# Attention scores: the low part of the keys stored on all 128 partitions

## The chip, the core and the metric

One Trainium2 chip, one of its cores. The metric is the device time of one execution in microseconds. The engines named below are TensorE (PE, its weight loads are listed apart as PEld), VectorE (DVE), ScalarE (ACT), GpSimd (POOL), and SyncE (SP), whose queue issues most of the loads from memory.

## The reference, cut to what matters

Two layers, 256 latent and 256 context tokens of width 1024. Each layer projects the tokens, runs three token mixers (attention, convolution, pooling) side by side, merges them, and ends in a mixture of 16 experts. The part of interest is the score product of the attention, with 8 query heads in two groups of 4, each group sharing one of 2 key heads of size 64:

```
s_win = jnp.einsum('bnqkgd,bnskd->bnkgqs', qb, kw)     # latent queries, latent keys in a band
s_ctx = jnp.einsum('bnqkgd,blkd->bnkgql', qb, k_ctx)   # latent queries, context keys
s     = jnp.einsum('blkgd,bmkd->bkglm', qg, k)         # context queries, context keys (layer 0 only)
```

All of it is in float32, and a softmax with one extra "sink" column follows.

## The kernel before

Products that need more accuracy than one pass of TensorE's fast float32 form gives are made from split operands. A value x is kept as a high part (x rounded to that form) and a low part (x minus the high part). The projections (helper `mm3`, lines 492 to 499) are three passes over such halves, eight matmuls each, all with weights of 128 rows.

For the scores a trick is used, since a head has only 64 dimensions and the array has 128 rows. In the tile of queries, `QS` for the latent and `QC` for the context tokens, 64 partitions of a head hold the high part of q and the other 64 hold its low part (lines 544 to 549). `KS` holds the high part of the keys twice, once on each half (lines 560 and 561). One matmul over all 128 rows so adds q_high times k_high and q_low times k_high. The low part of the keys, `KL`, is written by line 562 on the 64 partitions of its key head alone; a second matmul, with the 64 rows of q_high as weights, adds q_high times k_low.

`scores(s, qb, kv)` does one group of 4 heads for 128 queries. For context queries (s = 1) a head takes a pair of matmuls with 256 columns, lines 591 and 592. For latent queries (s = 0) it takes a triple: lines 596 and 597 with 512 columns, and line 598, a 128x128 bf16 product that adds the mask. Each result goes to one of four PSUM banks called `ax`; DVE takes the row maximum (601) and the softmax offset (603), ACT the exponential (606). `weigh` then scales the probabilities (624 on ACT, 626 on DVE) and transposes them on PE (631, evicted by 633), and `values` multiplies by v (644, 648, 649).

Layer 0 has 4 groups with s = 1 and 4 groups with s = 0, so 16 pairs and 16 triples; layer 1 has 4 groups with s = 0, so 16 triples. Between `scores` and `weigh` of a group the program puts one or two units of the convolution's projection (`conv_units`, lines 496 to 499) and some taps of the convolution on DVE (`pump_taps`, lines 474 and 478). A scheduler then sets the order on each engine, with the splits of the weights (lines 238 and 239) drawn ahead by a priority. Each engine works through its list in that order.

After the mixers come the output projection (872), the routing and the experts (1080, 1103, 1108). Their weights, 12 MB for each expert, are loaded by SP's queue into tiles as these come free (`prefetch`, line 355).

Of the kernel before, what the change touches and what calls it, by code (L numbers as in the profile page):

```python
# [10 lines left out]
F32 = mybir.dt.float32  # L11
F32R = mybir.dt.float32r
# [7 lines left out]
NH, NKV, HD, WIN = 8, 2, 64, 128  # L20
# [107 lines left out]
def dit_block(ctx: ExitStack, tc: tile.TileContext, out, kcv, kb16, rope_in, tok, cols, w_mod0, w_mod,  # L128
              b_mod, w_in, w_attn_o, w_conv_o, w_pool, w_pool_o, w_out, w_router,
              w_e, final_norm_g):  # L130
    nc = tc.nc

    def opened(name, bufs, side="left", **kw):
        g = tc.tile_pool(name=name, bufs=bufs, side=side, reuse_waits="tile", **kw)
        return g, g.__enter__()
# [9 lines left out]
    def bank(tag, dt=F32):  # L145
        pool, bufs = psum[tag]
        return pool.tile([128, 512], dt, tag=tag, name=tag, bufs=bufs)
# [19 lines left out]
    def t2(name, n=512, dt=F32):  # L167
        return L.tile([128, n], dt, tag="t2", name=name, bufs=6)
# [32 lines left out]
    def small(shape, name, bufs=2, dt=F32):  # L201
        return P0.tile(shape, dt, tag=name, name=name, bufs=bufs)
# [8 lines left out]
    for l in range(DEPTH):  # L211
# [8 lines left out]
        gdr, DR = opened(f"dr{l}", 1, side="right")  # L220
# [280 lines left out]
        def unit(src, n, view="p (k n) -> p k n", eng="v", **kw):  # L501
            w = split(src, view, eng, **(kw or dict(k=8)))
            w = [v.rearrange("p (k n) -> p k n", k=8) for v in w]
            ps = bank("mm")
            mm3(ps[:, :n], w, (hh, hl), 8, n)
            nunit[0] += 1
            if nunit[0] % MOD_EVERY[l] == 0:
                pump_mod()
            return ps
# [4 lines left out]

        QS = DR.tile([128, NH, 256], F32R, tag="qf", name="QS")
        KS = DR.tile([128, NKV, 512], F32R, name="KS")
        KL = DR.tile([128, 512], F32R, name="KL")
        if NS == 2:
            QC = big("E", "QC", F32R)[:, :2048].rearrange("p (h n) -> p h n", h=NH)
        sides = (slice(0, 64), slice(64, 128))  # L520
# [12 lines left out]
        for u in range(2):  # L533
            tv = qw.pop() if qw else qload(u)
            for v in range(2):
# [8 lines left out]
                for kv in range(2):  # L544
                    hp, ho = sides[kv], sides[1 - kv]
# [9 lines left out]
        kf = t2("kf")  # L555
        roped(kf[:, 0:256], ps)
        nc.scalar.activation(kf[:, 256:512], ps[:, 256:512], AF.Copy)
        for kv in range(2):
            hp, ho = sides[kv], sides[1 - kv]
            nc.scalar.activation(KS[hp, kv, :], kf[hp], AF.Copy)  # L560
            nc.vector.tensor_copy(KS[ho, kv, :], kf[hp])
            nc.vector.tensor_sub(KL[hp], kf[hp], KS[hp, kv, :].bitcast(F32))
        ps = unit(kvw[:, :, 128:256], 512, eng=LOW["v"][l])
        vf = t2("vf", 512)
        nc.scalar.activation(vf, ps, AF.Copy)
# [5 lines left out]
        def prt(name):  # L571
            return DR.tile([128, 2 * 272], F32, tag="pr", name=name, bufs=4)
# [7 lines left out]
        def scores(s, qb, kv):  # L580
            nk = 4 if s == 0 else 2
            q0 = 128 * qb
            hp = sides[kv]
            nm = small([128, 4], "nm")
            rs = small([128, 4], "rs")
            pr4 = []
            for i in range(4):
                sc = bank("ax")
                if s == 1:
                    q = QC[:, 4 * kv + i, q0:q0 + 128]  # L590
                    nc.tensor.matmul(sc[:, :256], q, KS[:, kv, 256:512], start=True, stop=False)
                    nc.tensor.matmul(sc[:, :256], q[hp], KL[hp, 256:512], start=False, stop=True)
                else:
                    kb = 1 - qb
                    q = QS[:, 4 * kv + i, q0:q0 + 128]
                    nc.tensor.matmul(sc, q, KS[:, kv, :], start=True, stop=False)
                    nc.tensor.matmul(sc, q[hp], KL[hp], start=False, stop=False)
                    nc.tensor.matmul(sc[:, kb * 128:(kb + 1) * 128], identb, maskb[:, qb, :],
                                     start=False, stop=True)
                mx = small([128, 1], "mx")  # L600
                nc.vector.reduce_max(mx, sc[:, :nk * 128], axis=AX.X)
                hs = 4 * kv + i
                nc.vector.tensor_scalar(nm[:, i:i + 1], mx, -(HD ** -0.5), nsink[:, hs:hs + 1],
                                        op0=ALU.mult, op1=ALU.min)
                pr = prt("pr")
                nc.scalar.activation(pr[:, :nk * 128], sc[:, :nk * 128], AF.Exp, scale=HD ** -0.5,
                                     bias=nm[:, i:i + 1], accum_out=rs[:, i:i + 1])
                pr4.append(pr)
            hs = 4 * kv
            es = small([128, 4], "es")  # L610
            nc.vector.tensor_add(es, nm, sink[:, hs:hs + 4])
            nc.scalar.activation(es, es, AF.Exp)
            nc.vector.tensor_add(rs, rs, es)
            nc.vector.reciprocal(rs, rs)
            return pr4, rs
# [62 lines left out]
        for s in reversed(range(NS)):  # L678
            for qb in range(2):
                if s == 0:  # L680
                    pT = A[1:]
                else:
                    p1 = A[2]
                    pT = [p1[:, :1024], p1[:, 1024:]]
                pT = [p.rearrange("p (k i n) -> p k i n", i=4, n=128) for p in pT]
                for kv in range(2):
                    pr4, rs = scores(s, qb, kv)
                    for _ in range(2 // NS):
                        next(fill, None)
                        pump_taps(TAPS["attn"][l])  # L690
                    weigh(s, kv, pT, pr4, rs)
                values(s, qb, pT)
# [340 lines left out]
        for e in range(NE):  # L1033
# [36 lines left out]
            for i in range(4):  # L1070
                wg, wu = [eload().rearrange("p (k n) -> p k n", k=2) for _ in range(2)]
                for kk in range(2):
                    k = 2 * i + kk
                    for f in range(2):
                        for u, w in enumerate((wg, wu)):
                            if NS == 2:
                                o = pgu[f][64 * u:64 * u + 64, :]
                            else:
                                o = pgu[0][64 * u + 32 * f:64 * u + 32 * f + 32, :]
                            nc.tensor.matmul(o, xeT[k // 4][:, k % 4, e, :], w[:, kk, 512 * f:512 * f + 512],  # L1080
                                             start=k == 0, stop=k == 7)
# [118 lines left out]
```

## Time and profile before

| | |
|---|---|
| median of 3 runs | 1712.94 us (1711.73 to 1713.78) |
| the profiled execution | 1712.34 us, its span 1710.5 us |
| PE busy | 1483.2 us (87%), 7788 matmuls |
| DVE busy | 670.3 us (39%) |
| ACT busy | 407.6 us (24%) |
| DMA, mean over the span | 310 GB/s |
| mean granted clock of TensorE | 0.941 |

A busy PE is not a PE at its peak: a matmul's record begins when it is given to the array and its end is modelled, so the gap between the starts of two neighbours says more than a record's own length. The attention of layer 0 stands at about 82 to 190 us of the span, that of layer 1 at about 1022 to 1081 us.

### The profile page before, as it was taken

How to read it: one execution, taken by the hardware profiler on the slowest of the kernel's cores; microseconds unless marked ns; L12 is line 12 of the kernel's file. 1: busy time of each engine (PE TensorE's matmuls, PEld its weight loads, DVE VectorE, ACT ScalarE, POOL GpSimd, SP SyncE). 2: the span in 40 equal slices, each digit the busy share in tenths (PEclk: the TensorE clock that was granted, in tenths of full speed). 3: DMA queues.
4: the chain of work that ended last, by engine and by line, in shares of the span. 5: the costliest groups of instructions: out<-in, count | busy, mean ns of one | idle time of the engine just before them, and what ended most of it. 6: DMA issues, size and time to landing. Idle time of an engine off the chain costs nothing. (4 is left out here: it accounts for less than half of the span.)

```text
span 1710.5 us, 19121 instructions
## 1 busy us (share of the span) xinstructions
PE 1483.2 (87%) x7788; PEld 802.1 (47%) x7788; DVE 670.3 (39%) x1137; ACT 407.6 (24%) x760; POOL 232.4 (14%) x234
## 2 busy tenths in 40 slices
PE   6999989999999999999998899999979765666575
PEld 3665667888654433333332267789844111111111
DVE  3568993352553221121211268975542110111011
ACT  3455312232432100000000257434421000000001
POOL 0300430154740000000000020325100000000000
PEclk9999999999999999999999999999989887878878
DMA  9643435234546999999999865566689999999996
GB/s 398 230 173 130 148 144 207 75 139 181 197 176 255 425 428 427 428 426 428 428 407 428 334 242 179 196 225 229 268 336 429 427 429 427 428 427 428 428 428 258
DMA packets 48185, 530.01 MB, mean 310 GB/s; under 512 B 5345, under 2 KB 6113, under 8 KB 7906
## 3 DMA queue, kind: packets, MB, share of 16 engines
q1 hardware_dynamic: 46224, 526.10, 75.8%
q10 hardware_dynamic: 1874, 2.70, 0.5%
q8 instruction: 61, 1.00, 0.2%
q14 instruction: 26, 0.21, 0.0%
HBM read 527.73 MB, written 1.05 MB: 309 GB/s over the span
## 5 line engine op out<-in xcount | busy, mean ns | idle before, releaser
L1080 PE MATMUL mm<-we,xeT 128*32 128x512 f32 (+1 forms) x1880 | 347.1, 662 | 97.8 <-DMA we<-in_w_e_dram 97.8
L1080 PEld LDWEIGHTS mm<-we,xeT 128*32 128x32 f32 (+1 forms) x1880 | 95.1, 129 | 337.5 <-issue 190.2
L496 PE MATMUL mm<-hh,ws 128*128 128x512 f32 (+1 forms) x672 | 221.8, 349 | 0.3
L497 PE MATMUL mm<-hl,ws 128*128 128x512 f32 (+1 forms) x672 | 218.6, 344 | 0.5 <-DVE hl L430 0.4
L238 ACT ACTIVATE ws<-w 128x1024 fp32r<-128x1024 f32 x132 | 139.3, 1058 | 303.6 <-PE mm L499 202.5
L1087 DVE TENSOR_TENSOR hm<-si,mm 64x512 f32<-64x512 f32 x48 | 33.1, 690 | 405.8 <-ACT si L1085 271.4
L1085 ACT ACTIVATE si<-mm 64x512 f32<-64x512 f32 x48 | 28.3, 590 | 684.9 <-PE mm L1080 684.9
L478 DVE SCALAR_TENSOR_TENSOR acc<-up,dw,acc 128x512 f32<-128x512 f32 (+1 forms) x240 | 156.7, 693 | 1.1
L239 DVE TENSOR_TENSOR ws<-w,ws 128x1024 fp32r<-128x1024 f32 x94 | 122.3, 1304 | 70.5 <-ACT ws L238 70.2
L496 PEld LDWEIGHTS mm<-hh,ws 128*128 128x128 f32 x672 | 127.3, 190 | 29.2 <-issue 12.6
L497 PEld LDWEIGHTS mm<-hl,ws 128*128 128x128 f32 x672 | 127.4, 190 | 18.6 <-issue 3.5
L499 PE MATMUL mm<-hh,ws 128*128 128x512 f32 (+1 forms) x672 | 132.7, 339 | 1.0 <-DVE ws L239 0.9
L239 POOL TENSOR_TENSOR ws<-w,ws 128x1024 fp32r<-128x1024 f32 x38 | 97.2, 2564 | 211.2 <-ACT ws L238 211.2
L1103 PE MATMUL mm<-we,hT 128*64 128x512 f32 x432 | 111.2, 639 | 5.0 <-ACT hT L1098 4.8
L499 PEld LDWEIGHTS mm<-hh,ws 128*128 128x128 f32 x672 | 107.1, 189 | 15.9 <-DVE ws L239 2.1
L1045 POOL COPY sel<-kc 48x128 f32<-48x128 f32 (+1 forms) x16 | 4.6, 285 | 799.8 <-DVE hm L1087 428.8
L1115 DVE TENSOR_TENSOR Y<-mm,G 32x512 f32<-32x512 f32 x64 | 44.0, 687 | 135.8 <-PE mm L1103 135.0
L1108 PE MATMUL mm<-we,hT 128*32 128x512 f32 x424 | 69.1, 762 | 11.6 <-DMA we<-in_w_e_dram 9.6
L1103 PEld LDWEIGHTS mm<-we,hT 128*64 128x64 f32 x432 | 33.5, 146 | 76.5 <-issue 66.1
L1125 PE MATMUL ax<-Y,sg 128*128 128x512 f32 x128 | 58.4, 603 | 8.8 <-DVE Y L1118 6.4
L1118 DVE TENSOR_TENSOR Y<-mm,G 64x512 f32<-64x512 f32 x32 | 22.0, 688 | 96.1 <-PE mm L1108 95.7
L1095 PE MATMUL ax<-kc,hm 64*128 64x64 f32 x192 | 32.6, 294 | 31.0 <-DVE hm L1087 30.2
(260 smaller groups left out, 1715.3 us busy)
## 6 DMA issues: line engine op xcount, KB each, us to landing
we<-in_w_e_dram SPq DMA_DIRECT2D x166, 2048.0 KB, 26.6
w<-in_w_mod_dram SPq DMA_DIRECT2D x44, 1024.0 KB, 5.3
w<-in_w_in_dram SPq DMA_DIRECT2D x42, 1024.0 KB, 4.9
A<-in_w_e_dram SPq DMA_DIRECT2D x20, 2048.0 KB, 23.2
w<-in_w_out_dram SPq DMA_DIRECT2D x12, 1024.0 KB, 4.9
we<-in_w_e_dram SPq DMA_DIRECT2D x10, 1024.0 KB, 17.3
wm<-in_w_mod_dram SPq DMA_DIRECT2D x4, 1024.0 KB, 18.0
w<-in_w_attn_o_dram SPq DMA_DIRECT2D x4, 1024.0 KB, 4.9
```

What stands on the lines that cost most here:

```text
L238: nc.scalar.activation(h, src, AF.Copy)
L239: (nc.gpsimd if eng == "p" else nc.vector).tensor_sub(lw, src, h.bitcast(F32))
L478: nc.vector.scalar_tensor_tensor(acc[:, ch], up[:, ch, :, k:k + 256], dw[:, 4 * k + ch:4 * k + ch + 1], acc[:, ch], op0=ALU.mult, op1=ALU.add)
L496: nc.tensor.matmul(ps, wh[:, k, :], ah[:, k, :n], start=k == 0, stop=False)
L497: nc.tensor.matmul(ps, wh[:, k, :], al[:, k, :n], start=False, stop=False)
L499: nc.tensor.matmul(ps, wl[:, k, :], ah[:, k, :n], start=False, stop=k == nk - 1)
L1080: nc.tensor.matmul(o, xeT[k // 4][:, k % 4, e, :], w[:, kk, 512 * f:512 * f + 512], start=k == 0, stop=k == 7)
L1087: nc.vector.tensor_mul(hm[0:64, :], si[0:64, :], pgu[f][64:128, :])
L1103: nc.tensor.matmul(pd[64 * h:64 * h + 64, :], hT[:, 64 * k:64 * k + 64], rhs, start=k == 0, stop=k == 7)
L1108: nc.tensor.matmul(pd[o:o + 32, :], hT[:, c0:c0 + 32], rhs, start=k < 2, stop=k >= 6)
L1115: nc.vector.tensor_mul(Y[b0:b0 + 32, s, cols], pd[rw, :], G2[l][rw, :])
L1125: nc.tensor.matmul(po, sgs[s][:, t * 128:(t + 1) * 128], Y[:, s, cols], start=True, stop=True)
```

## The change

`KL` becomes one 128-partition block for each key head. Line 562 writes the half it wrote before, a new line 563 writes the same difference on the other half, and both score matmuls of a head take the whole 128-row query tile as weights. The second product so adds q_low times k_low as well.

```
-        KL = DR.tile([128, 512], F32R, name="KL")
+        KL = DR.tile([128, NKV, 512], F32R, name="KL")
...
-            nc.vector.tensor_sub(KL[hp], kf[hp], KS[hp, kv, :].bitcast(F32))
+            nc.vector.tensor_sub(KL[hp, kv, :], kf[hp], KS[hp, kv, :].bitcast(F32))
+            nc.vector.tensor_sub(KL[ho, kv, :], kf[hp], KS[hp, kv, :].bitcast(F32))
...
-            hp = sides[kv]
...
-                    nc.tensor.matmul(sc[:, :256], q[hp], KL[hp, 256:512], start=False, stop=True)
+                    nc.tensor.matmul(sc[:, :256], q, KL[:, kv, 256:512], start=False, stop=True)
...
-                    nc.tensor.matmul(sc, q[hp], KL[hp], start=False, stop=False)
+                    nc.tensor.matmul(sc, q, KL[:, kv, :], start=False, stop=False)
```

On PE, ACT, POOL and SP the instructions stand in the order they had. DVE gets two more subtractions in each layer. In layer 0 they stand between the casts of the high keys (`KS`) and the split of the next weights (`ws`), as this piece of the difference of DVE's list shows (- before, + after):

```order
 L561 CAST KS<-kf 64x512 x2
-L562 TENSOR_TENSOR KL<-kf,KS 64x512 x2
-L239 TENSOR_TENSOR ws<-w,ws 128x1024
-L569 COPY vt<-ax 128x512
+L562 TENSOR_TENSOR KL<-kf,KS 64x512
+L563 TENSOR_TENSOR KL<-kf,KS 64x512
+L562 TENSOR_TENSOR KL<-kf,KS 64x512
+L563 TENSOR_TENSOR KL<-kf,KS 64x512
+L239 TENSOR_TENSOR ws<-w,ws 128x1024
+L570 COPY vt<-ax 128x512
```

Both halves of key head 0 are now written before the first of key head 1, and the split and the copy of v (`vt`) stand behind four subtractions in place of two.

In layer 1 no split stands between them and the copy of v, after which come the row maxima of the first scores; this is the same place of DVE's list there:

```order
 L239 TENSOR_TENSOR ws<-w,ws 128x1024
 L561 CAST KS<-kf 64x512 x2
-L562 TENSOR_TENSOR KL<-kf,KS 64x512 x2
-L569 COPY vt<-ax 128x512
+L562 TENSOR_TENSOR KL<-kf,KS 64x512
+L563 TENSOR_TENSOR KL<-kf,KS 64x512
+L562 TENSOR_TENSOR KL<-kf,KS 64x512
+L563 TENSOR_TENSOR KL<-kf,KS 64x512
+L570 COPY vt<-ax 128x512
```

The copy of v moves behind two more subtractions, and with it the maxima that follow.

## Rows read from the trace of the kernel before

**Rows 1.** Stretches: width; busy of PE, PEld, DVE, ACT, POOL; clock; DMA share, GB/s.
```profile
82.00:120.00 38.00, 38.00 (x171) 25.57 (x170) 25.64 (x68) 20.82 (x63) 0.00 (x0) 1.00 0.43 146
127.00:172.00 45.00, 43.74 (x208) 25.94 (x205) 38.42 (x74) 25.95 (x55) 2.39 (x1) 1.00 0.35 126
1020.00:1075.00 55.00, 55.00 (x359) 39.40 (x358) 45.48 (x105) 42.36 (x84) 0.15 (x2) 1.00 0.44 152
1400.00:1700.00 300.00, 194.91 (x1067) 47.00 (x1060) 39.62 (x59) 14.29 (x31) 2.43 (x5) 0.81 0.98 415
```

**Rows 2.** Chain that ended last, in order of time: start, us, what.
```profile
1023.79 0.43 PE ax L597
...
1651.84 37.13 DMA we<-in_w_e_dram
```

**Rows 3.** Groups by line, weight loads: busy, mean ns, idle before, what ended it.
```profile
L496 PEld LDWEIGHTS mm<-hh,ws 128*128 128x128 f32 x672 | 127.3, 190 | 29.2 <-issue 12.6 <-ACT ws L238 1.0 <-ACT pr L624 0.8
...
L597 PEld LDWEIGHTS ax<-KL,QS 64*128 64x128 f32 x32 | 5.8, 183 | 8.6 <-issue 8.6
...
L592 PEld LDWEIGHTS ax<-KL,QC 64*128 64x128 f32 x16 | 2.9, 183 | 2.5 <-issue 1.0
```

**Rows 4.** Timeline of PE, triples of layer 0: start, us, what.
```profile
128.45 0.50 PE L597 MATMUL ax<-KL,QS 64*128 64x512 f32 x1
128.88 0.23 PE L598 MATMUL ax<-bt 128*128 128x128 bf16 x1
128.92 0.48 PE L596 MATMUL ax<-KS,QS 128*128 128x512 f32 x1
129.33 0.50 PE L597 MATMUL ax<-KL,QS 64*128 64x512 f32 x1
...
131.74 0.23 PE L598 MATMUL ax<-bt 128*128 128x128 bf16 x1
131.78 0.48 PE L497 MATMUL mm<-hl,ws 128*128 128x512 f32 x1
132.09 0.39 PE L496 MATMUL mm<-hh,ws 128*128 128x512 f32 x1
132.32 0.40 PE L497 MATMUL mm<-hl,ws 128*128 128x512 f32 x1
```

**Rows 5.** Timeline of PE, pairs of layer 0.
```profile
91.96 0.38 PE L591 MATMUL ax<-KS,QC 128*128 128x256 f32 x1
92.27 0.38 PE L592 MATMUL ax<-KL,QC 64*128 64x256 f32 x1
92.58 0.38 PE L591 MATMUL ax<-KS,QC 128*128 128x256 f32 x1
```

**Rows 6.** Timeline of PE, a projection with 256 columns in layer 1.
```profile
1032.59 0.28 PE L497 MATMUL mm<-hl,ws 128*128 128x256 f32 x1
1032.71 0.28 PE L496 MATMUL mm<-hh,ws 128*128 128x256 f32 x1
```

**Rows 7.** Waits, DVE and PE in 127:172, PE in 172:235: us, times, longest.
```profile
DVE mx L601 <- PE ax L598: 3.3, 6, 1.4
...
PE ax L631 <- ACT pr L624: 1.3, 1, 1.3
...
PE mm L499 <- DVE ws L239: 4.9, 2, 4.2
```

**Rows 8.** Timeline of DVE where the subtractions stand, layers 0 and 1 [idle before].
```profile
77.33 1.41 DVE L562 TENSOR_TENSOR KL<-kf,KS 64x512 fp32r<-64x512 f32 x2
...
80.85 1.23 DVE L239 TENSOR_TENSOR ws<-w,ws 128x1024 fp32r<-128x1024 f32 x1 [2.12 <-ACT ws L238]
...
1022.72 0.69 DVE L569 COPY vt<-ax 128x512 f32<-128x512 f32 x1 [0.58 <-PE ax L568]
1023.54 0.69 DVE L601 TENSOR_REDUCE mx<-ax 128x1 f32<-128x512 f32 x1
```

**Rows 9.** Waits of SP's queue over the whole span: us, times, longest.
```profile
SPq L355 <- PE mm L1080: 294.1, 77, 26.3
```

## The prediction

> **What bounds the kernel now.** I read the stretches first, then the chain, then the timeline of PE inside the attention, then the waits.
>
> The table of stretches shows where the end is made. In the context part of the attention of layer 0 (82 to 120 us) and in the attention of layer 1 (1020 to 1075 us) PE is busy for every microsecond, and in 127 to 172 us for 43.74 of 45; the DMA engines are at 0.35 to 0.44 [rows 1]. Near the end it is the reverse: from 1400 to 1700 us the DMA engines are at 0.98 and PE is busy for 65% [rows 1]. The chain that ended last agrees: in layer 1 it runs through the score matmuls themselves (0.43 us of line 597 in each triple), at the end through the loads of expert weights [rows 2]. Those loads do not start at a fixed time: SP's queue waits 294 us in all for expert matmuls to free their tiles [rows 9]. So if everything ahead of the experts moves earlier, the first tiles come free earlier, and the string of loads moves with them. Time saved on PE in the attention should reach the end.
>
> Is PE slow there? A weight load of line 496, with 128 rows, takes 190 ns; there are 672, with 29.2 us of idle time ahead of them, 43 ns each. A load of line 597, with 64 rows, takes 183 ns and has 8.6 us ahead of 32, that is 269 ns each, all of it "issue": nothing the profile shows was waited for [rows 3]. The timeline says what that costs. Neighbours of equal height with 512 columns start 0.23 us apart (132.09 to 132.32), so the next load lies wholly beside the running product. From line 597 to line 598, from 64 rows to 128, it is 0.43 us; from line 596 to line 597 it is 0.41 [rows 4].
>
> **The change, part by part.** *The triples.* Before, one triple takes 129.33 - 128.45 = 0.88 us: 0.43 + 0.04 + 0.41. After, no weight in it changes height. The step 597 to 598 should take the 0.23 of equal neighbours. The 0.04 stays. The step 596 to 597 follows the short mask product, and the same step is there between matmuls of equal height: after line 598 at 131.74, line 497 starts 0.04 later and the next one 0.31 after that [rows 4]. Together 0.58, so 0.30 less. There are 32 triples, 16 in each layer: 4.8 us for each layer.
>
> *The pairs* of layer 0 with 256 columns: 0.31 to line 592 and 0.31 back to line 591, 0.62 a pair [rows 5]. Equal heights with 256 columns start 0.12 apart [rows 6], so 0.24 a pair, 0.38 less. 16 pairs: 6.1 us.
>
> The sum on PE is 6.1 + 4.8 + 4.8 = 15.7 us. No row shows a full-height score pair, so both ends: nothing at all, if the wait has another cause than the height; and 18.3 us, if the triple falls to 0.23 + 0.23 + 0.04 = 0.50 (32 x 0.38 = 12.2, plus 6.1). I take 15.7, since it is made of steps that the trace shows between neighbours of equal height.
>
> *The added subtractions.* Line 562 takes 1.41 us for two, so 0.7 each [rows 8]; four more, two in a layer, are 2.8 us on DVE. In layer 0 the next instruction is the split of a weight, and it stands idle for 2.12 us, waiting for ACT [rows 8]; 1.4 us fit in, and the cover is that wait. In layer 1 the copy of v comes next, with 0.58 us idle; it starts about 0.8 us later, and the first row maximum, which has 0.1 us to spare behind the copy, about 0.6 late [rows 8]. The four maxima then come without gaps, where before they waited for PE, so most of this is made up inside the group. Queued behind are the group's softmax and one split; the transposes that need the softmax stand behind two units of projection. If that cover is gone, 0.6 to 1.4 us of layer 1 are lost. I book 0.4. Both halves of key head 0 are done first, so the second matmul of the first pair does not wait for head 1.
>
> *What is late next.* A group's softmax on DVE and ACT must be done when PE comes to the transposes, and PE now comes 1.2 us earlier in each group of triples and 1.5 in each group of pairs. In 127 to 172 us DVE is busy for 38.4 of 45 us [rows 1], and PE waits once for the softmax, 1.3 us [rows 7]. Where PE is already waiting, the gain must come through DVE. It can: in this stretch DVE itself waits 3.3 us, in 6 places, for score products [rows 7], and these gaps close when a triple takes 0.58 in place of 0.88, since the maximum of one head alone takes DVE 0.69 us [rows 8]. Later PE waits 4.9 us for a split behind the taps on DVE, in 172 to 235 us [rows 7]: the split, too, must come earlier, not only PE. I take off 1.3 us in layer 0 for gaps of DVE that do not close.
>
> In sum: 15.7 - 0.4 - 1.3 = 14.0 us. From the profiled execution, 1712.34 us (span 1710.5 and 1.8 around it), that gives 1698.3; the median of the runs is 0.6 above this execution, so 1698.9.
>
> **Rivals.**
> *DVE takes back the latent part.* If DVE, busy for 85% in 127 to 172 us, cannot move forward between groups, PE gains only in the pairs (6.1) and about half in layer 1, where DVE is busy for 45.48 of 55 us plus 1.4 added (2.4 more): 8.5 us, 1704.4. For it: the waits of PE on softmax and split [rows 7]. Against it: DVE's own gaps are waits for PE.
>
> *The height is not the reason.* Then nothing is gained and the subtractions mostly hide: 1712.9 to 1714. For it: the second product differs from the first in its key tile as well. Against it: lines 496 and 497 differ in that too, and their loads hide. The Trainium skill says that a load's time goes by columns and not rows, a 32-row load taking as long as a 128-row one ("TensorE: Matmul & The Clock Gate", section on LDWEIGHTS). By that alone the time would be the 1713 of this rival. The trace agrees on the length, 183 against 190 ns, but the 269 ns ahead of the 64-row load are what the page leaves open [rows 3].
>
> *Slower: full-height loads cannot pass the product before them.* A load of 64 rows touches half the array, a load of 128 rows all of it. If it had to wait for the running product to leave, each step of 512 columns would cost what 597 to 598 costs now, 0.43, and a triple 0.43 + 0.43 + 0.12 (what the mask product adds to equal neighbours today: 0.04, and 0.31 in place of 0.23 behind it) = 0.98, that is 0.10 more; 32 of them are 3.2 us, the pairs stay at 0.62, and up to 2.8 us of subtractions lose their cover: 6.0 us, so about 1719. It decides once 596 to 597 takes more than 0.44 us. Against it: 128-row loads follow each other at 0.23 all through the projections [rows 4]. The Trainium skill has this rule on the same page, section "The mechanism": a weight load overlaps running matmuls only when its row group differs. By that rule 1719; the trace disagrees, since loads of 190 ns on equal rows lie inside steps of 230 ns [rows 3, 4].
>
> *The loads hide it.* If the experts' loads ended when they do now, the time would stay at 1713. Against it: they wait for tiles [rows 9].
>
> **How the numbers follow.** The forecast has 0.78 (its own range 1694.6, with the whole 18.3, to 1702). DVE taking part of it back: 0.10. Height not the reason: 0.06. Loads hide it: 0.03. Slower: 0.03. A measurement of this kernel can tell about 0.2%, 3.4 us, from no change. The first two are faster, 0.87 with a little of the third's spread taken off; no change about 0.10; slower by more than 0.2% the 0.03. The range of 8 in 10 goes from 1694.5 to 1707: it holds the forecast, all of the first rival but its weak end, and leaves out no change.
>
> **What would show it.** In the changed kernel the loads of line 597 should have about 50 ns of idle time ahead of them in place of 269, neighbours 597 and 598 should start 0.23 us apart, triples 0.58 and pairs 0.24. The attention of layer 0 should end about 9.6 us earlier, and layer 1 should add about 4.4 to that. The last load should land 14 us earlier. Line 631's wait for the softmax should stay near its 1.3 and the wait of line 499 near 4.9; if they grow by several microseconds, the first rival holds. The prediction is wrong if the steps stay at 0.4, or if PE's gain at 190 us is gone at 300.

## The result, and the profile after

The changed kernel takes 1699.13 us (median; 1696.53 to 1701.63), beside 1713.36 us for the kernel before on the same chip: a ratio of 0.9918, 95% interval 0.9897 to 0.9939. That is 14.2 us less. The forecast was 14.0 us, at 1698.9. The profiled execution took 1699.61 us, its span 1697.8.

The two kinds of group first. The height of a product is the number of rows, 64 or 128, that its weights take. This is the timeline of PE in layer 0 after the change (start, us, line): a stretch of triples, then one of pairs.

```profile
121.95 0.23 PE L598 MATMUL ax<-bt 128*128 128x128 bf16 x1
121.99 0.47 PE L596 MATMUL ax<-KS,QS 128*128 128x512 f32 x1
122.31 0.40 PE L597 MATMUL ax<-KL,QS 128*128 128x512 f32 x1
122.55 0.23 PE L598 MATMUL ax<-bt 128*128 128x128 bf16 x1
122.59 0.47 PE L596 MATMUL ax<-KS,QS 128*128 128x512 f32 x1
```

```profile
89.67 0.28 PE L591 MATMUL ax<-KS,QC 128*128 128x256 f32 x1
89.79 0.28 PE L592 MATMUL ax<-KL,QC 128*128 128x256 f32 x1
89.91 0.28 PE L591 MATMUL ax<-KS,QC 128*128 128x256 f32 x1
```

A triple is 0.04 + 0.32 + 0.24 = 0.60 us, where it was 0.88 [rows 4]; the step 597 to 598 fell from 0.43 to 0.24. A pair is 0.24 us, where it was 0.62 [rows 5].

The same in the weight loads (columns as in [rows 3]):

```profile
L597 PEld LDWEIGHTS ax<-KL,QS 128*128 128x128 f32 x32 | 6.1, 191 | 0.9 <-issue 0.8
...
L592 PEld LDWEIGHTS ax<-KL,QC 128*128 128x128 f32 x16 | 3.0, 189 | 0.0
```

The load of line 597 is 8 ns longer than before and has 28 ns of idle time ahead of it in place of 269. Idle time ahead of a load is not a cost by itself, though: the mask's load has 269 ns ahead of it too (8.6 us for 32), beside a running product, and the step from line 597 to it is 0.24 us all the same.

```profile
L598 PEld LDWEIGHTS <-bt 128*128 128x128 bf16 x32 | 3.1, 97 | 8.6 <-issue 8.4
```

Next, the place of the saving. I take two marks on either side of each attention: the casts of the high keys (line 561), and the first products after the mixers (line 853). The rows give the first and the last start of each over the span; here before, then after. Layer 0 is counted from the first cast to the first product, layer 1 from the last cast to the last product.

```profile
L561 DVE CAST KS<-kf x4: 422/423/423, 76.4 to 1020.3; 64x512 fp32r<-64x512 f32 x4
...
L853 PE MATMUL ax<-GM,kc x12: 590/592/696, 435.0 to 1220.0; 128*128 128x512 f32 x12
```

```profile
L561 DVE CAST KS<-kf x4: 421/423/423, 75.9 to 1011.4; 64x512 fp32r<-64x512 f32 x4
...
L853 PE MATMUL ax<-GM,kc x12: 590/592/696, 424.5 to 1206.0; 128*128 128x512 f32 x12
```

Layer 0 takes 358.6 us between its marks before and 348.6 after: 10.0 less. Layer 1 takes 199.7 and 194.6: 5.1 less in these two executions. Work without the change lies between: from the second mark of layer 0 to the first of layer 1 it is 585.3 us before and 586.9 after.

Those 1.6 us have a visible cause. The table of stretches (columns as in [rows 1]) shows it, in the output projection of layer 0; first before, then after, each 15 us wide around the same work.

```profile
475.00:490.00 15.00, 12.56 (x72) 8.83 (x70) 12.04 (x28) 6.46 (x10) 9.97 (x5) 1.00 0.22 72
```

```profile
464.50:479.50 15.00, 12.83 (x67) 9.28 (x65) 10.44 (x28) 5.60 (x10) 8.34 (x4) 0.89 0.22 71
```

The granted clock is 1.00 before and 0.89 after. In both executions PE stands idle for 2.17 us there, waiting for DVE in the routing. Behind the same wait the products of line 872 run at full clock before, but not after:

```profile
478.37 0.38 PE L934 MATMUL ax<-kc,rex 128*16 128x128 f32 x2 [2.17 <-DVE rex L931]
478.51 1.18 PE L872 MATMUL mm<-ws,mh 128*128 128x512 f32 x4
479.52 1.08 PE L872 MATMUL mm<-ws,ml 128*128 128x512 f32 x4
...
482.26 1.07 PE L872 MATMUL mm<-ws,ml 128*128 128x512 f32 x4
```

```profile
467.92 0.38 PE L934 MATMUL ax<-kc,rex 128*16 128x128 f32 x2 [2.17 <-DVE rex L931]
468.05 1.55 PE L872 MATMUL mm<-ws,mh 128*128 128x512 f32 x4
469.41 1.91 PE L872 MATMUL mm<-ws,ml 128*128 128x512 f32 x4
...
473.41 1.07 PE L872 MATMUL mm<-ws,ml 128*128 128x512 f32 x4
```

The sixteen products ahead of the last row take 473.41 - 468.05 = 5.36 us after and 482.26 - 478.51 = 3.75 before, 1.6 us apart: for a part of them the clock is at its lower level (1.2 GHz in place of 2.4; the granted clock in 470 to 472 us is 0.50). A second run of the changed kernel has the same wait and not the fall; its first two groups of four take 1.03 and 0.92 us, where they took 1.01 and 0.92 before, and 584.5 us lie between its marks of layers 0 and 1. Of the ten profiled executions behind this document five show the fall, among them that of the kernel with the subtractions alone, which gains nothing. So this is a scatter of single executions, not an effect of the change.

Last, what the softmax and the loads do. The waits of DVE in 116 to 161 us, which holds the work of 127 to 172 before, and then those of PE in 82 to 172 and in 172 to 235 us (us, times, longest):

```profile
DVE mx L601 <- PE ax L598: 1.5, 2, 1.1
```

```profile
PE ax L631 <- ACT pr L624: 1.3, 1, 1.3
...
PE mm L499 <- DVE ws L239: 4.9, 2, 4.2
```

DVE's wait for scores fell from 3.3 us to 1.5, while PE's waits for the softmax and for the split stayed where they were [rows 7]. Over 82 to 250 us, a stretch that holds both in either kernel, PE waits 5.2 us for splits and 3.0 for the softmax before, 4.9 and 3.1 after (5.3 and 3.1 in the second run of the changed kernel). DVE moved forward together with PE.

```profile
1010.93 0.88 DVE L561 CAST KS<-kf 64x512 fp32r<-64x512 f32 x2 [0.63 <-POOL kf L531]
...
1013.94 0.69 DVE L563 TENSOR_TENSOR KL<-kf,KS 64x512 fp32r<-64x512 f32 x1
1014.55 0.68 DVE L570 COPY vt<-ax 128x512 f32<-128x512 f32 x1
1015.15 1.27 DVE L601 TENSOR_REDUCE mx<-ax 128x1 f32<-128x512 f32 x2
```

That is the timeline of DVE in layer 1 after the change. The copy of v follows the subtractions with no gap, and the maxima follow it. Counted from the cast, the copy comes 3.62 us later, where it was 2.89 [rows 8, with the cast at 1019.83], 0.7 late; the last pair of maxima ends 7.1 us after the cast now (at 1018.07) and 7.0 before. The lateness on DVE is made up inside the group.

### The profile page after: what moved, and what is told of

Its sections match the earlier page's. It is cut to its first block, busy times and chain, and to the rows that moved or that the text cites. A ratio compares the mean times of both kernels' runs of the same rounds, so it can differ in the third digit from the quotient of the medians.

```text
span 1697.8 us, 19127 instructions
## 1 busy us (share of the span) xinstructions
PE 1469.8 (87%) x7788; PEld 797.6 (47%) x7788; DVE 673.0 (40%) x1141; ACT 407.1 (24%) x760; POOL 231.1 (14%) x234
## 4 chain that ended last, share of the span: by engine, by line
PE 38%; DMA 27%; DVE 4%; issue 2%; ACT 1%; POOL 1%; POOLq 0%; ACTq 0%; DVEq 0%; SPq 0%
DMA we<-in_w_e_dram 24%; PE mm L1080 11%; PE mm L1103 6%; PE mm L987 3%; PE mm L872 3%; PE mm L497 2%; PE mm L496 2%; PE mm L499 2%; DMA A<-in_w_e_dram 2%; PE ax L1125 2%; DVE acc L478 1%; PE mm L1108 1%; PE ax L1095 1%; PE md L255 1%; DVE ws L239 1%
```

## The experiments

Each run was compared with the kernel before on the same chip, which was measured three times: 1713.36 us goes with the first run of the changed kernel, 1714.05 with the four runs from "pairs alone" to "other full-height weights", 1713.82 with the rest. The table gives the ratio to it, and the time between the marks of each layer in the profiled execution.

| kernel | median us | ratio, 95% interval | layer 0 | layer 1 |
|---|---|---|---|---|
| before | 1713.36, 1714.05, 1713.82 | 1 | 358.6 | 199.7 |
| changed | 1699.13 | 0.9918 (0.9897 to 0.9939) | 348.6 | 194.6 |
| changed, again | 1699.65 | 0.9922 (0.9899 to 0.9944) | 348.1 | 196.7 |
| pairs alone | 1709.39 | 0.9975 (0.9963 to 0.9988) | 353.0 | 198.7 |
| triples alone | 1703.72 | 0.9946 (0.9932 to 0.9959) | 354.6 | 193.5 |
| subtractions alone | 1713.37 | 0.9993 (0.9981 to 1.0006) | 359.1 | 198.8 |
| other full-height weights | 1699.46 | 0.9912 (0.9897 to 0.9928) | 348.1 | 195.5 |
| both products 64 rows | 1709.11 | 0.9975 (0.9962 to 0.9988) | 353.6 | 198.9 |
| subtraction on GpSimd | 1699.90 | 0.9924 (0.9904 to 0.9944) | 348.7 | 193.9 |
| subtraction three times | 1701.89 | 0.9942 (0.9920 to 0.9964) | 349.0 | 196.5 |

The first three runs take the change apart.

**Pairs alone**

```
-                    nc.tensor.matmul(sc, q, KL[:, kv, :], start=False, stop=False)
+                    nc.tensor.matmul(sc, q[hp], KL[hp, kv, :], start=False, stop=False)
```

Here and in the next runs `hp` stands for the 64 partitions of the key head; the line that sets it is not shown.

> The changed kernel, but the second product of the latent triples has 64-row weights again; only the 16 context pairs of layer 0 are full-height. All subtractions stay. If the height change costs by the step: 16 x 0.38 = 6.1 us of PE, so about 5.5 us below the kernel before (ratio 0.9968), pairs 0.24 us, triples 0.88. If the gain came from the triples only: no change.

Measured: 0.9975 of the kernel before, 4.3 us less by the ratio; in layer 0, the only one with pairs, 5.6 us less. The pairs take 0.24 us, the triples 0.88, as expected.

**Triples alone**

```
-                    nc.tensor.matmul(sc[:, :256], q, KL[:, kv, 256:512], start=False, stop=True)
+                    nc.tensor.matmul(sc[:, :256], q[hp], KL[hp, kv, 256:512], start=False, stop=True)
```

> The changed kernel, but the second product of the context pairs has 64-row weights again; only the 32 latent triples are full-height. If the height change costs by the step: 32 x 0.29 = 9.3 us of PE, about 9 us below the kernel before (ratio 0.9947), triples 0.59 us, pairs 0.62. If DVE holds the latent part back: 4 us or less. The gains of this run and of the pairs alone should add up to that of the whole change, 14.

Measured: 0.9946, 9.3 us less; 4.0 us in layer 0 and 6.2 in layer 1. The triples take 0.59 us, the pairs 0.62. The gains of the two runs add up to 13.5 us by the ratios. The whole change gives 13.4 to 14.0 in the same way, in its two comparisons.

**Subtractions alone**: both edits above together, so that only the layout of the low keys and the four subtractions remain.

> The low keys are stored on all 128 partitions with the four added subtractions, but both kinds of second product use 64-row weights as before. If the gain is the height alone: 0 to 1.4 us slower than the kernel before (ratio 1.0000 to 1.0008). If the layout of the tile itself helps: faster by some us.

Measured: 0.9993, its interval holds 1; layer 0 is 0.5 us longer. Against this run, in layer 0, the pairs give 6.1 us, the triples 4.5, and both 10.5 to 11.0. The forecast had 6.1 and 4.8 ahead of deductions. For layer 1 the five profiles with full-height triples and the single subtractions (changed, again, triples alone, other weights, GpSimd) lie at 193.5 to 196.7 with a mean of 194.8, the three with 64-row second products and 128-row first ones at 198.7 to 199.7 with a mean of 199.1: 4.2 us less, though the five alone are spread over 3.2 us.

**Other full-height weights** asks whether it is that the weights of a pair are equal in height, or that they are the same weights. The second product takes the queries of the next head, so the low part of the keys meets the wrong head.

```
-                    nc.tensor.matmul(sc, q, KL[:, kv, :], start=False, stop=False)
+                    q2 = QS[:, 4 * kv + (i + 1) % 4, q0:q0 + 128]
+                    nc.tensor.matmul(sc, q2, KL[:, kv, :], start=False, stop=False)
```

The pairs are edited in the same way, with `QC`.

> The second product of each head takes the full-height queries of the next head of its group as weights, so the two products of a pair have equal height but different weights; the low part of the keys is thus multiplied with the wrong head. If equal height is the reason: the time of the changed kernel, 1699 us, pairs 0.24 and triples 0.59 us. If it is that the weights of the pair are the same and a load is spared: the gain shrinks or goes, 1706 to 1713 us.

Measured: 0.9912, the whole gain. The timeline of PE in this run (line 599 is its second product, 600 its mask):

```profile
122.81 0.23 PE L600 MATMUL ax<-bt 128*128 128x128 bf16 x1
122.85 0.47 PE L597 MATMUL ax<-KS,QS 128*128 128x512 f32 x1
123.16 0.40 PE L599 MATMUL ax<-KL,QS 128*128 128x512 f32 x1
123.40 0.23 PE L600 MATMUL ax<-bt 128*128 128x128 bf16 x1
```

A triple takes 0.59 us with other weights, too. Equal weights have no part in it.

**Both products 64 rows** asks whether 64 rows are slow as such, or the change from one height to the other. Both products use q_high alone (q_low times k_high is left out).

```
-                    nc.tensor.matmul(sc, q, KS[:, kv, :], start=True, stop=False)
-                    nc.tensor.matmul(sc, q, KL[:, kv, :], start=False, stop=False)
+                    nc.tensor.matmul(sc, q[hp], KS[hp, kv, :], start=True, stop=False)
+                    nc.tensor.matmul(sc, q[hp], KL[hp, kv, :], start=False, stop=False)
```

The pairs likewise.

> Both products of a head use the 64 rows of q_high as weights (q_low times k_high is left out), the four subtractions stay. If any change of height costs and equal heights do not: inside a group the pairs fall to 0.24 us as with full height, and only the borders to the 128-row projections are paid, some 8 of them, 0.4 us each: about 4 us below the kernel before. The triples keep two changes, since the mask product has 128 rows: 0.88 us, no gain. If it is the 64-row weights themselves that are slow: pairs at 0.62 or more and no gain at all.

Measured: 0.9975, 4.3 us less. PE's timeline: two pairs of a group and the borders to a projection and back (592 and 593 are the pair, 496 has 128 rows), then a triple (597, 598, mask 599). The third piece is the same place in the changed kernel, where 591 and 592 are the pair and all have 128 rows.

```profile
82.75 0.27 PE L592 MATMUL ax<-KS,QC 64*128 64x256 f32 x1
82.87 0.28 PE L593 MATMUL ax<-KL,QC 64*128 64x256 f32 x1
82.99 0.28 PE L592 MATMUL ax<-KS,QC 64*128 64x256 f32 x1
83.10 0.28 PE L593 MATMUL ax<-KL,QC 64*128 64x256 f32 x1
83.31 0.49 PE L496 MATMUL mm<-hh,ws 128*128 128x512 f32 x1
83.73 0.38 PE L592 MATMUL ax<-KS,QC 64*128 64x256 f32 x1
```

```profile
125.00 0.49 PE L597 MATMUL ax<-KS,QS 64*128 64x512 f32 x1
125.33 0.39 PE L598 MATMUL ax<-KL,QS 64*128 64x512 f32 x1
125.66 0.23 PE L599 MATMUL ax<-bt 128*128 128x128 bf16 x1
125.82 0.49 PE L597 MATMUL ax<-KS,QS 64*128 64x512 f32 x1
```

```profile
82.18 0.28 PE L592 MATMUL ax<-KL,QC 128*128 128x256 f32 x1
82.30 0.39 PE L496 MATMUL mm<-hh,ws 128*128 128x512 f32 x1
82.54 0.38 PE L591 MATMUL ax<-KS,QC 128*128 128x256 f32 x1
```

Among themselves, matmuls with 64-row weights and 256 columns start 0.12 us apart, exactly as 128-row ones do. With 512 columns the step from 597 to 598 is 0.33, beside 0.32 at full height (596 to 597). Only at the borders do the steps rise: from 593 to 496 to 0.21, where the changed kernel has 0.12, and from 496 back to 592 to 0.42, where it has 0.24. So 64 rows are not slow; changing is. The expectation for the triples missed: 0.82 us, not 0.88. Compared with the 0.60 of full height, the steps into the mask (0.33 for 0.24) and out of it (0.16 for 0.04) are longer, 0.09 and 0.12. One change so costs 0.09, 0.12 or 0.18 us here, where the triples of the kernel before paid 0.28 for two and the pairs 0.38. The price of one change is thus 0.1 to 0.2 us, depending on what stands on either side; why it differs, no run here tells.

The last runs ask what the added work on DVE costs.

**Subtraction on GpSimd**

```
-            nc.vector.tensor_sub(KL[ho, kv, :], kf[hp], KS[hp, kv, :].bitcast(F32))
+            nc.gpsimd.tensor_sub(KL[ho, kv, :], kf[hp], KS[hp, kv, :].bitcast(F32))
```

> The changed kernel with the two added subtractions of each layer on GpSimd in place of DVE. If DVE's added 2.8 us cost 0.4 us as booked: 1699 us, at most 0.5 below the changed kernel, not to be told from it. If they cost their full 1.4 us in layer 1: 1.4 below. If the subtraction takes over 2 us on GpSimd and the first scores wait for it: 1 to 4 us above.

**Subtraction three times**

```
-            nc.vector.tensor_sub(KL[ho, kv, :], kf[hp], KS[hp, kv, :].bitcast(F32))
+            for _ in range(3):
+                nc.vector.tensor_sub(KL[ho, kv, :], kf[hp], KS[hp, kv, :].bitcast(F32))
```

> The changed kernel with the added subtraction done three times: four more of 0.69 us on DVE in each layer, 2.75 us a layer. If DVE has cover there: layer 0 loses 0.7 to 1.3 us (the 2.12 us ahead of the split now hold 4.1), layer 1 up to 2.7, together 1 to 4 us above the changed kernel, 1700 to 1703. If DVE sets the pace of both layers from there on: 5.5 us above, 1704.6.

**The changed kernel again**

> The changed kernel once more, for the comparison within this call: 1699 us, 0.992 of the kernel before.

Measured: 1699.90 us on GpSimd and 1699.65 again, 0.9924 and 0.9922: not to be told apart, so moving them gains nothing. It does not give the price of the added work, though, for DVE did not get its time back. The run's groups of lines 562 and 563:

```profile
L562 DVE TENSOR_TENSOR KL<-kf,KS 64x512 fp32r<-64x512 f32 x4 | 6.7, 1666 | 0.1
L563 POOL TENSOR_TENSOR KL<-kf,KS 64x512 fp32r<-64x512 f32 x4 | 5.9, 1467 | 1.6 <-ACT KS L560 1.5
```

Beside the subtractions of GpSimd, DVE's own four take 1.67 us each in place of 0.69, 6.7 us together, where the changed kernel spends 5.5 on all eight. The price is bounded by the run with the subtractions alone: its interval ends at 1.0006, so ahead of the old second products the four added ones cost at most about 1 us.

With three times as many, 1701.89 us, 2.2 above the changed kernel run beside it; the intervals of the two ratios overlap, so the 2.2 us are not clear of noise. The profile shows why some price is now to be expected. Its timeline of DVE in layer 0, the wait of PE there, and its group of line 598 (the second product; the wait is in layer 1) read:

```profile
79.43 2.84 DVE L564 TENSOR_TENSOR KL<-kf,KS 64x512 fp32r<-64x512 f32 x4
82.30 1.23 DVE L239 TENSOR_TENSOR ws<-w,ws 128x1024 fp32r<-128x1024 f32 x1
```

```profile
PE ax L592 <- DVE vt L571: 0.8, 1, 0.8
...
L598 PE MATMUL ax<-KL,QS 128*128 128x512 f32 x32 | 12.8, 407 | 1.2 <-DVE KL L564 1.2
```

The split of the weights no longer waits ahead of its turn: its 2.12 us of idle time [rows 8], 0.73 of which were left in the changed kernel, are used up. PE waits 0.8 us for the copy of v in layer 0 and 1.2 us for the low keys in layer 1; in the changed kernel it has neither wait. In layer 0 the cover was there and was about as large as the rows showed; the change itself stays inside it.

No run was faster than the changed kernel by more than its interval.

## Why the prediction was right

- *Bound by PE in the attention, and the loads follow.* Shown: 14.2 us less at the end, and the last product of the expert stage (line 1080) starts 12.9 us earlier in the profile, beside 14.0 at the last mark of line 853. SP's last string of issues of expert loads ends at 1645.90 us where it was 1659.95, 14 us earlier as foretold. The chain of the changed kernel still runs through the expert loads near its end, from 1297 us on where it was from 1313. The loads moved with their tiles, and the rival in which they hide the gain is out.
- *The height is the reason.* Shown from both sides: equal weights are not needed (other full-height weights gave the whole gain), full height is not needed (64-row neighbours with 256 columns start 0.12 us apart), and the layout of the low keys alone gives nothing.
- *The terms.* Pairs 0.38 us each: measured 0.62 - 0.24. Triples 0.30 each: measured 0.88 - 0.60 = 0.28. By these steps PE saves 15.0 us, 0.7 less than the 15.7 of the forecast. In layer 0 the forecast was 9.6 us after deductions; the profiles show 10.0 to 10.5. In layer 1 it was 4.4; the runs show 4.2 as a difference of means.
- *The deductions.* 1.3 us in layer 0 for gaps of DVE was too much: of the 10.6 us that the measured steps give there (6.1 + 4.5), 10.0 to 10.5 arrive, and the waits of PE for the softmax and the split did not grow. The 0.4 us for the added subtractions cannot be told from nothing. So the steps were taken 0.7 us too large and the deduction 0.7 to 1.2 us, and the two errors met. That the forecast of 14.0 lies 0.2 from the measured 14.2 is luck: the interval of the ratio reaches from 10.5 to 17.6 us, and the clock alone scattered single executions by 1.6.
- *Rivals.* DVE taking back the latent part: out, the triples alone gave 9.3 us, where this rival left them 2.4. Slower, with loads that cannot pass the product before them: out, loads of 189 to 191 ns on all rows stand beside steps of 0.24 us with 512 columns, and with 256 columns the step, 0.12 us, is shorter than the load itself. This is against the rule of the Trainium skill ("TensorE: Matmul & The Clock Gate", section "The mechanism"), as the rows of before had said. Another page of the Trainium skill, "TensorEngine Tiling (Array Packing)", section "Key Properties", says that changing the tiling mode, not just the tile, drains the array. The trace agrees in that a change costs 0.1 to 0.2 us and equal heights nothing; that it is a drain, no run here shows.

## What to carry to other kernels

Read the gap between the starts of neighbouring matmuls, not their records: a product with 64-row weights between 128-row ones took 0.28 to 0.38 us longer for its two changes of height than with a harmless extra term on the other 64 rows. Where half of the array's rows are idle in one product of a chain, fill them so that the height stays the same, if the copy can be made once and used by many products: here eight subtractions in all, 5.5 us of DVE, half of them there before, serve 48 score products. Where every product of a stretch has 64 rows, nothing is gained by filling: both kinds step by 0.12 us with 256 columns.

## What the runs showed of the hardware that was not expected

- One change of height costs about 0.1 us or about 0.2, depending on its neighbours: 0.09 and 0.12 around the mask product between 64-row products, 0.09 from a 64-row pair to a projection and 0.18 from a projection to such a pair, 0.28 for the two changes of a triple before, 0.38 for the two of a pair.
- Idle time of 269 ns ahead of the mask's weight load went with a step of 0.24 us in the changed kernel, where equal neighbours take 0.23; the same 269 ns ahead of the 64-row load went with triples 0.28 us longer.
- After one and the same wait of 2.15 to 2.17 us on PE the granted clock fell to its lower level in five profiled executions and not in five others; the fall cost 1.6 us of 1700.
- Beside subtractions of the same shape on GpSimd (1.47 us each) DVE's took 1.67 us, where they take 0.69 otherwise; no run here tells why.
